# Two norm factors from running sums, and the work around them, in a hybrid decoder step on one core

## The chip, the cores and the metric

The kernel runs on one core of a Trainium2 chip. Its time is the device time of one execution in microseconds (us). A core has five engines with queues of their own: TensorE (PE in the rows, its weight loads PEld), VectorE (DVE), ScalarE (ACT), GpSimd (POOL) and SyncE (SP, which here only issues DMAs). Each engine takes its instructions in the order of its queue.

## The reference

One layer for 256 prompt tokens and 64 sample tokens (8 sequences of 8), 320 tokens of width 2048 in all, in fp32. Cut to what matters here:

```python
merged = sigmoid(gate_a) * y_a + sigmoid(gate_b) * y_b
x  = x + gt1 * rms_norm(merged @ w_o, g_post_mix)
h2 = rms_norm(x, g_pre_mlp) * (1.0 + sc2) + sh2
u  = relu(h2 @ w_up)
x  = x + gt2 * rms_norm((u * u) @ w_down, g_post_mlp)
# rms_norm(x, g): x * rsqrt(mean(x * x) + 1e-6) * g
# sh1, sc1, gt1, sh2, sc2, gt2: six parts of silu(c) @ w_ada + b_ada, for each sequence
```

Between `merged @ w_o` and `h2 @ w_up` there are two norms, one after the other: the first gives a factor r for each token (over the product with `w_o`), and the second a factor r2 (over the new x, which holds r).

## The kernel before

Activations lie transposed, with channels on the 128 partitions and the 320 tokens along a row. A matrix product is made by `gemm`: 256 output channels at a time into two PSUM banks of the pool `acc` (four banks), with 8 blocks of 128 input channels to one DMA of 1 MB (`load_w`, on SP, three buffers `raw`). Each half of such a load is split into a high part (`whi`, ScalarE) and the rest (`wlo`, VectorE), three buffers each, and each block takes three matmuls (`mm3`), so that a group of 16 blocks is 96 matmuls of 320 columns.

The order of every engine's queue is fixed when the kernel is built, by a planner that weighs its own estimates of time and the order of the program text. `tc.issue_after(ins)` keeps the instructions of a block behind `ins`, where they are on the same engine as `ins`; it bears on no other engine.

**The adaLN parts** (`ada_gen`, `ada_steps`) come in 96 steps of one 1 MB load and 8 matmuls with 32 columns of weights (`aux<-raw,cT`). After each fourth step the sums are copied (`adarow`, ScalarE), turned by four transposes and reduced (`ada_turn`). 14 of the 96 steps are left when the product with `w_o` ends. All 14 belong to `gt2`, which is not needed before the last part of the MLP. 10 of them are called in one row behind the product with `w_o`, with loads into the pool `fraw` (three buffers); the others are called by `tick` in the MLP.

**The end of the mixer.** For each of the eight groups of `w_o`, `out_squares` squares the two blocks and adds them to `ssum`, `out_tile` multiplies by `gt1` (`zg`) and turns the blocks by transposes into two PSUM banks of the pool `aux`, and `out_store` copies them to `zt` (tokens on partitions: two tiles of 128 prompt tokens, one of 64 sample tokens). The sums of squares are those of the product before `gt1` and the gain. Behind the last group `tok_rstd` adds `ssum` over the partitions with matmuls and gives r (`rstd_of`: Ln and Exp on ScalarE, then one Newton step of four small instructions on VectorE).

**Between mixer and MLP.** Six instructions make `x1 = zt * r + x1` on VectorE, 1024 wide, and ScalarE squares each half behind it with a running sum. From the six sums comes r2. `h2_scale` then multiplies blocks of 256 channels by r2 into `zt` on VectorE. A loop over eight pairs of channel blocks turns each by transposes (`aux<-ident,zt`), applies scale and shift (`h2t`, ScalarE, VectorE and GpSimd), and splits it into `gh` and `gl`, the inputs of the product with `w_up`.

**The end.** In the last of eight rounds of the MLP, each group of `w_down` is added to `za` and goes through the same `out_squares`, `out_tile` and `out_store`. `tok_rstd` gives the last r, and twelve instructions on VectorE (512 wide, L1417) make the result, each followed by its output DMA on SP's or ScalarE's queue.

## Time and profile before

| | |
|---|---|
| time, median of 3 runs | 2158.01 us (2155.7 to 2158.17) |
| time of the profiled execution | 2156.86 us |
| its span, first to last instruction | 2155.0 us |
| what lies around the span | 1.86 us |
| mean granted TensorE clock | 0.990 of full speed |
| TensorE busy | 97% of the span |
| VectorE, ScalarE, GpSimd busy | 50%, 40%, 8% |
| DMA | 401.69 MB, mean 186 GB/s |

Times inside the trace are us from the start of the span. A busy share is the share of the time in which an engine has an instruction under way; matmuls are pipelined, and the length of one (0.31 us) is longer than the distance between two (0.147 us). The granted clock of 1.00 is 2.4 GHz and 0.50 is 1.2 GHz.

### The profile page before, as it was taken

The page shows a single profiled execution, that of the slowest core. Times are in us where ns is not written, and L with a number is a line of the kernel's source. Part 1 is how long each engine was busy: PE and PEld are TensorE (multiplying, and loading weights), DVE is VectorE, ACT ScalarE, POOL GpSimd, SP SyncE. Part 2 cuts the span into 40 slices and gives each one's busy share as a digit, 9 for nine tenths or more (in the row PEclk, how much of TensorE's full clock was granted, in tenths as well). Part 3 has the DMA queues.
Part 4 walks back from the last instruction along what each step waited for, and adds up shares of the span by engine and source line. Part 5 has one row for each costly group of instructions (what it writes and reads, how often), then busy time and mean ns, then how long its engine had stood idle before and what let it go on. Part 6 is the DMA issues. An engine that isn't in the chain of part 4 may idle for free.

```text
span 2155.0 us, 34660 instructions
## 1 busy us (share of the span) xinstructions
PE 2098.8 (97%) x14605; PEld 1899.2 (88%) x14605; DVE 1077.7 (50%) x1673; ACT 863.4 (40%) x1312; POOL 165.5 (8%) x167
## 2 busy tenths in 40 slices
PE   6999998999999999999999899999999999999997
PEld 4788988557878889999999599999999999999996
DVE  3655754446765645533544643444444444444455
ACT  5322443334545434333343543434343333333343
POOL 0000100203221211000010000000000000000001
PEclk9999999999999999999999799999999999999998
DMA  9876544544766768766854565445445445445442
GB/s 310 313 268 235 195 169 130 217 129 139 241 214 225 243 208 280 227 208 203 274 178 137 180 189 176 152 145 157 145 149 156 144 150 157 143 151 157 142 152 70
DMA packets 327572, 401.69 MB, mean 186 GB/s; under 512 B 10984, under 2 KB 265528, under 8 KB 324600
## 3 DMA queue, kind: packets, MB, share of 16 engines
q1 hardware_dynamic: 301576, 362.82, 52.4%
q0 software_dynamic: 3584, 21.50, 2.8%
q10 hardware_dynamic: 22256, 15.16, 2.3%
q8 instruction: 115, 1.88, 0.4%
q14 instruction: 41, 0.34, 0.1%
HBM read 387.44 MB, written 12.01 MB: 185 GB/s over the span
## 4 chain that ended last, share of the span: by engine, by line
PE 87%; issue 4%; DVE 4%; DMA 3%; ACT 1%; SPq 1%; POOL 0%; DVEq 0%; ACTq 0%; POOLq 0%
PE acc L136 76%; PE aux L136 7%; PE aux L139 4%; DVE wlo L148 1%; DMA raw<-in_w_ada_dram 1%; DMA raw<-in_w_in_dram 1%; ACT whi L151 1%; DMA raw<-in_w_q_up_dram 1%; SPq L161 0%; DVE zu L1417 0%; DVE X L148 0%; DMA raw<-in_w_kv_up_dram 0%; POOL qt L142 0%; DVE zg L142 0%; DVE bb L967 0%
## 5 line engine op out<-in xcount | busy, mean ns | idle before, releaser
L148 DVE TENSOR_TENSOR wlo<-raw,whi 128x1024 fp32r<-128x1024 f32 (+1 forms) x493 | 604.1, 1231 | 709.1 <-ACT whi L151 708.4
L151 ACT CAST whi<-raw 128x1024 fp32r<-128x1024 f32 (+1 forms) x493 | 503.0, 1026 | 817.9 <-PE acc L136 680.5
L136 PE MATMUL acc<-hh,whi 128*128 128x320 f32 x1168 | 369.6, 317 | 2.8 <-ACT hh L151 1.5
L136 PE MATMUL acc<-hl,whi 128*128 128x320 f32 x1168 | 361.9, 310 | 0.0
L136 PE MATMUL acc<-hh,wlo 128*128 128x320 f32 x1168 | 361.7, 311 | 0.0
L136 PE MATMUL acc<-uh,whi 128*128 128x320 f32 x1024 | 316.7, 309 | 0.0
L136 PE MATMUL acc<-gh,whi 128*128 128x320 f32 x1024 | 316.7, 309 | 0.0
L136 PE MATMUL acc<-gh,wlo 128*128 128x320 f32 x1024 | 316.6, 309 | 0.0
L136 PE MATMUL acc<-gl,whi 128*128 128x320 f32 x1024 | 316.3, 309 | 0.0
L136 PE MATMUL acc<-uh,wlo 128*128 128x320 f32 x1024 | 316.1, 309 | 0.0
L136 PE MATMUL acc<-ul,whi 128*128 128x320 f32 x1024 | 316.1, 309 | 0.0
L136 PEld LDWEIGHTS acc<-hh,whi 128*128 128x128 f32 x1168 | 219.4, 188 | 34.8 <-issue 18.6
L136 PEld LDWEIGHTS acc<-hh,wlo 128*128 128x128 f32 x1168 | 219.1, 188 | 3.0 <-DVE wlo L148 1.7
L136 PEld LDWEIGHTS acc<-hl,whi 128*128 128x128 f32 x1168 | 219.7, 188 | 2.0 <-DVE hl L148 1.2
L136 PEld LDWEIGHTS acc<-gh,whi 128*128 128x128 f32 x1024 | 192.5, 188 | 1.9 <-ACT u L1387 0.8
L136 PEld LDWEIGHTS acc<-uh,whi 128*128 128x128 f32 x1024 | 192.6, 188 | 1.7 <-ACT u L1386 0.8
L136 PEld LDWEIGHTS acc<-gh,wlo 128*128 128x128 f32 x1024 | 192.6, 188 | 0.2
L136 PEld LDWEIGHTS acc<-gl,whi 128*128 128x128 f32 x1024 | 192.6, 188 | 0.0
L136 PEld LDWEIGHTS acc<-ul,whi 128*128 128x128 f32 x1024 | 192.4, 188 | 0.0
L136 PEld LDWEIGHTS acc<-uh,wlo 128*128 128x128 f32 x1024 | 192.4, 188 | 0.0
L136 PE MATMUL aux<-raw,cT 128*32 128x512 f32 (+1 forms) x832 | 116.2, 603 | 16.6 <-DVE tt L142 11.3
L145 POOL TENSOR_TENSOR ssum<-ssum,sqt 128x320 f32<-128x320 f32 x26 | 25.9, 997 | 981.2 <-ACT sqt L1267 980.3
(425 smaller groups left out, 2551.1 us busy)
## 6 DMA issues: line engine op xcount, KB each, us to landing
raw<-in_w_ada_dram SPq DMA_DIRECT2D x96, 1024.0 KB, 6.1
raw<-in_w_up_dram SPq DMA_DIRECT2D x64, 1024.0 KB, 5.7
raw<-in_w_down_dram SPq DMA_DIRECT2D x64, 1024.0 KB, 5.3
raw<-in_w_in_dram SPq DMA_DIRECT2D x60, 1024.0 KB, 5.5
raw<-in_w_o_dram SPq DMA_DIRECT2D x16, 1024.0 KB, 5.3
raw<-in_w_in_dram SPq DMA_DIRECT2D x20, 512.0 KB, 6.2
raw<-in_w_b_out_dram SPq DMA_DIRECT2D x8, 1024.0 KB, 6.4
raw<-in_w_a_out_dram SPq DMA_DIRECT2D x8, 1024.0 KB, 5.5
```

What stands on the lines that cost most here:

```text
L136: pe_last[0] = nc.tensor.matmul(out, lhsT=lhsT, rhs=rhs, start=start, stop=stop)
L139: pe_last[0] = nc.tensor.transpose(out=out, in_=in_, identity=ident[:k, :k])
L145: (eng or nc.vector).tensor_tensor(out=out, in0=a, in1=b, op=ALU.add)
L148: return (eng or nc.vector).tensor_tensor(out=out, in0=a, in1=b, op=ALU.subtract)
L151: nc.scalar.copy(out=hi, in_=src)
```

## The change

The second norm needs the sum of (x + r z)² over the channels, where z is the gated product. The changed kernel gets it as sum x² + 2 r sum xz + r² sum z². Sum x² is kept from the first norm of the layer (`xms`). `out_sums` forms the other two in each group of `w_o`, straight from the PSUM banks: three products on VectorE with a reduction, and three squares on ScalarE with a running sum. So r2 follows from r by a few instructions that are three columns wide, and the residual `x1` is made in blocks of 256 channels inside `h2_scale`, behind r2; the scaling of two of its three tiles goes to ScalarE. `h2_scale` runs one pair ahead and not two.

In the last group of `w_o` and of `w_down`, `gemm` finishes the one output block before it takes up the other (`apart`), and the last block's squares are not added to `ssum` but go into the sum over partitions by three more matmuls. Of the ten adaLN steps, three stand behind the product with `w_o` (their matmuls behind those of r), four in the loop over the pairs, and three more than before in the MLP. `behind_of` keeps their copies and reductions behind the norm's instructions, and the first weight splits of `w_up` (VectorE's half) behind r2. At the end, the samples' addition is made by TensorE: the identity times x1 plus a diagonal matrix of r times z in PSUM, which ScalarE copies out; VectorE keeps the eight prompt instructions. All prompt outputs go out on SP's queue and the samples' on ScalarE's.

```diff
+    def behind_of(i):
+
+        return tc.issue_after(i.ins) if i is not None else nullcontext()
...
-    def gemm(w2d, kt0, nkt, c0, xh, xl, fine=False):
+    def gemm(w2d, kt0, nkt, c0, xh, xl, fine=False, apart=False, floor=None):
 
         ps = [bank(acc), bank(acc)]
         for r0 in range(0, nkt, 8):
             raw, rv = load_w(w2d, kt0 + r0, 8, c0, 256)
+            if apart and r0 == nkt - 8:
+                sp = [split_w(rv, 4 * s, 4, 256) for s in range(2)]
+                for m in range(2):
+                    ms = slice(m * P, (m + 1) * P)
+                    for k in range(8):
+                        hv, lv = sp[k // 4]
+                        mm3(ps[m][:, 0:N], hv[:, k % 4, ms], lv[:, k % 4, ms], xh[:, r0 + k], xl[:, r0 + k],
+                            r0 + k == 0, k == 7)
+                tick()
+                continue
             for s in range(2):
-                hv, lv = split_w(rv, 4 * s, 4, 256)
+                with behind_of(floor if r0 + s else None):
+                    hv, lv = split_w(rv, 4 * s, 4, 256)
...
+            with behind_of(pinned[0]):
+                nc.vector.tensor_reduce(out=m9[:, 0:nb], axis=AX.X, op=ALU.add,
+                                        in_=p2[:, 0:nb * P].rearrange("p (j g u) -> p j u g", g=4, u=32)[:, :, 0:9])
...
+                    with behind_of(after_mm[0]):
+                        mm(ps[32 * (k % 4):32 * (k % 4 + 1), 0:nb * P], cT[:, r0 + k], rv[:, k], r0 + k < 4, r0 + k >= KF - 4)
...
+                    with behind_of(pinned[0]):
+                        nc.scalar.copy(out=row[:, 0:nb * P], in_=ps[:, 0:nb * P])
...
+            if f == KF - 1:
+                return t
...
-    def tok_rstd(pl, ssum):
+    def tok_rstd(pl, blocks):
+
         ps = bank()
-        for i, t0, n in TOK:
-            mm(ps[0:n, i:i + 1], ssum[:, t0:t0 + n], ones[:, 0:1], True, True)
         xx = pl.tile([P, 3], F32, name="trx")
         tm = pl.tile([P, 3], F32, name="trt")
         r = pl.tile([P, 3], F32, name="trr")
         nc.vector.memset(xx, 1.0)
-        mean_eps(xx[:, 0:2], ps[:, 0:2], D)
-        mean_eps(xx[0:NS, 2:3], ps[0:NS, 2:3], D)
+        for j, sq in enumerate(blocks):
+            for i, t0, n in TOK:
+                mm(ps[0:n, 3 * j + i:3 * j + i + 1], sq[:, t0:t0 + n], ones[:, 0:1], True, True)
+            for n, c0, c1 in ((P, 0, 2), (NS, 2, 3)):
+                if j == 0:
+                    mean_eps(xx[0:n, c0:c1], ps[0:n, c0:c1], D)
+                else:
+                    nc.vector.scalar_tensor_tensor(out=xx[0:n, c0:c1], in0=ps[0:n, 3 + c0:3 + c1], scalar=1.0 / D,
+                                                   in1=xx[0:n, c0:c1], op0=ALU.mult, op1=ALU.add)
...
+        prod = zp.tile([P, 3, 256], F32, name="prod")
+        zsq = zp.tile([P, 256], F32, name="zsq")
+        cz = zp.tile([P, 2, 3, 9], F32, name="cz")
+        nc.vector.memset(prod, 0.0)
+        nc.vector.memset(cz, 0.0)
+
+        def out_sums(bk, g, m0, m1, col):
+
+            fs = slice((2 * g + m0) * P, (2 * g + m1) * P)
+            w = slice(0, (m1 - m0) * P)
+            for i, t0, n in TOK:
+                v = bk[0][:, m0:m1, i] if i < 2 else bk[1][0:NS, m0:m1]
+                xv, pv, qv = (t.rearrange("p (m c) -> p m c", c=P) for t in
+                              (x1[i][0:n, fs], prod[0:n, i, w], zsq[0:n, w]))
+                mul(pv, v, xv)
+                nc.scalar.activation(out=qv, in_=v, func=AF.Square, accum_out=cz[0:n, 1, i, col:col + 1])
+            nc.vector.tensor_reduce(out=cz[:, 0, :, col], in_=prod[:, :, w], axis=AX.X, op=ALU.add)
...
-            ps = gemm(w_o, 0, KF, 256 * g, mh, ml)
+            last = g == 7
+            ps = gemm(w_o, 0, KF, 256 * g, mh, ml, apart=last)
             bk = out_banks()
             for m in range(2):
-                out_squares(zp2, ps[m][:, 0:N], 2 * g + m, ssum)
-            for m in range(2):
-                out_tile(zp2, ps[m][:, 0:N], 2 * g + m, m, GT1, bk)
+                lsq = out_squares(zp2, ps[m][:, 0:N], 2 * g + m, ssum)
+                if last and m:
+                    r = tok_rstd(zp, (ssum, lsq))
+                    r_exp, after_mm[0] = last_exp[0], pe_last[0]
+                if last or m:
+                    for mm_ in range(m if last else 0, m + 1):
+                        out_tile(zp2, ps[mm_][:, 0:N], 2 * g + mm_, mm_, GT1, bk)
+                if last:
+                    out_sums(bk, g, m, m + 1, 7 + m)
...
-        r = tok_rstd(zp, ssum)
+            if not last:
+                out_sums(bk, g, 0, 2, g)
+        pinned[0] = r_exp
         araw[0] = fraw
-        for _ in range(10):
+        for _ in range(3):
             next(ada_steps)
-        araw[0] = wraw
-        ssq2 = zp.tile([P, 3, 2], F32, name="ssq2")
+        after_mm[0] = None
+
+        cs = zp.tile([P, 2, 3], F32, name="cs")
         xx2 = zp.tile([P, 3], F32, name="xx2")
         r2 = zp.tile([P, 3], F32, name="r2")
         t2_ = zp.tile([P, 3], F32, name="t2_")
-        nc.vector.memset(ssq2, 0.5)
-        for i, t0, n in TOK:
-            for j in range(2):
-                fs = slice(j * D // 2, (j + 1) * D // 2)
-                nc.vector.scalar_tensor_tensor(out=x1[i][0:n, fs], in0=zt[i][0:n, fs], scalar=r[0:n, i:i + 1],
-                                               in1=x1[i][0:n, fs], op0=ALU.mult, op1=ALU.add)
-                nc.scalar.activation(out=zt[i][0:n, fs], in_=x1[i][0:n, fs], func=AF.Square,
-                                     accum_out=ssq2[0:n, i, j:j + 1])
-        add(xx2, ssq2[:, :, 0], ssq2[:, :, 1])
-        mean_eps(xx2, xx2, D)
-        rstd_of(xx2, t2_, r2)
+        nc.vector.tensor_reduce(out=cs, in_=cz, axis=AX.X, op=ALU.add)
+        mul(xx2, cs[:, 1], r)
+        nc.vector.scalar_tensor_tensor(out=xx2, in0=cs[:, 0], scalar=2.0, in1=xx2, op0=ALU.mult, op1=ALU.add)
+        mul(xx2, xx2, r)
+        nc.vector.scalar_tensor_tensor(out=xx2, in0=xx2, scalar=1.0 / D, in1=xms, op0=ALU.mult, op1=ALU.add)
+        nc.vector.tensor_scalar(out=xx2, in0=xx2, scalar1=EPS, scalar2=None, op0=ALU.max)
+        r2_last = rstd_of(xx2, t2_, r2)
+        pinned[0] = r2_last
...
-                nc.vector.tensor_scalar(out=zt[i][0:n, fs], in0=x1[i][0:n, fs], scalar1=r2[0:n, i:i + 1], scalar2=None,
-                                        op0=ALU.mult)
+                with behind_of(r2_last):
+                    nc.vector.scalar_tensor_tensor(
+                        out=x1[i][0:n, fs], in0=zt[i][0:n, fs], scalar=r[0:n, i:i + 1], in1=x1[i][0:n, fs],
+                        op0=ALU.mult, op1=ALU.add)
+                if i == 0:
+                    nc.vector.tensor_scalar(out=zt[i][0:n, fs], in0=x1[i][0:n, fs], scalar1=r2[0:n, i:i + 1],
+                                            scalar2=None, op0=ALU.mult)
+                else:
+                    nc.scalar.activation(out=zt[i][0:n, fs], in_=x1[i][0:n, fs], func=AF.Copy, scale=r2[0:n, i:i + 1])
 
         h2_scale(0)
-        h2_scale(2)
...
-            if q0 + 4 < KF:
-                h2_scale(q0 + 4)
+            if q0 + 2 < KF:
+                h2_scale(q0 + 2)
...
+            if q0 % 4 == 2:
+                next(ada_steps)
+        pinned[0] = None
+        araw[0] = wraw
...
-                ps = gemm(w_up, 0, KF, c * 1024 + 256 * g, gh, gl)
+                ps = gemm(w_up, 0, KF, c * 1024 + 256 * g, gh, gl, floor=r2_last if c + g == 0 else None)
...
-                ps = gemm(w_down, 8 * c, 8, 256 * g, uh, ul)
+                ps = gemm(w_down, 8 * c, 8, 256 * g, uh, ul, apart=last and g == 7)
...
-                        out_squares(ml2, za[:, f], f, ssum)
+                        lsq = out_squares(ml2, za[:, f], f, ssum)
+                        if f == KF - 1:
+                            r = tok_rstd(ml1, (ssum, lsq))
+                        out_tile(ml2, za[:, f], f, m, GT2, bk)
                 if last:
-                    for m in range(2):
-                        out_tile(ml2, za[:, 2 * g + m], 2 * g + m, m, GT2, bk)
                     out_store(bk, zt, g)
-        r = tok_rstd(ml1, ssum)
+
+        ysb = [bank(acc) for _ in range(4)]
+        for q in range(4):
+            mm(ysb[q][0:NS], ident[0:NS, 0:NS], x1[2][0:NS, q * 512:(q + 1) * 512], True, False)
+        dg = ml1.tile([NS, NS], F32, name="dg")
+        nc.scalar.activation(out=dg, in_=ident[0:NS, 0:NS], func=AF.Copy, scale=r[0:NS, 2:3])
         for q in range(4):
             fs = slice(q * 512, (q + 1) * 512)
-            for i, t0, n in TOK:
+            mm(ysb[q][0:NS], dg, zt[2][0:NS, fs], False, True)
+            for i, t0, n in TOK[0:2]:
                 nc.vector.scalar_tensor_tensor(
                     out=zt[i][0:n, fs], in0=zt[i][0:n, fs], scalar=r[0:n, i:i + 1],
                     in1=x1[i][0:n, fs], op0=ALU.mult, op1=ALU.add)
-                dst = y_prompt[0, t0:t0 + n, fs] if i < 2 else y_sample.rearrange("b t d -> (b t) d")[:, fs]
-                (nc.sync if i % 2 else nc.scalar).dma_start(out=dst, in_=zt[i][0:n, fs])
+                nc.sync.dma_start(out=y_prompt[0, t0:t0 + n, fs], in_=zt[i][0:n, fs])
+            nc.scalar.copy(out=zt[2][0:NS, fs], in_=ysb[q][0:NS])
+            nc.scalar.dma_start(out=y_sample.rearrange("b t d -> (b t) d")[:, fs], in_=zt[2][0:NS, fs])
```

`out_squares` and `out_store` are otherwise as before; in the groups 0 to 6 `out_sums` stands behind `out_store`. `rstd_of` now returns its last instruction, and in the first norm of the layer `ssq` is replaced by `xms`, which outlives it.

## Rows read from the trace of the kernel before

**Rows 1.** The page's busy time, share of the span and instructions of each engine.
```profile
PE 2098.8 (97%) x14605; PEld 1899.2 (88%) x14605; DVE 1077.7 (50%) x1673; ACT 863.4 (40%) x1312; POOL 165.5 (8%) x167
```

**Rows 2.** Timeline, w_o to MLP: start us, us, engine, line, instruction, count, idle before.
```profile
1185.43 0.31 PE L136 MATMUL acc<-mh,wlo 128*128 128x320 f32 x1
...
1191.22 1.06 PE L136 MATMUL aux<-raw,cT 128*32 128x512 f32 x8
...
1191.97 7.25 DVE L1334 SCALAR_TENSOR_TENSOR x<-zt,trr,x 128x1024 f32<-128x1024 f32 x6
...
1200.32 1.94 PE L136 MATMUL aux<-raw,cT 128*32 128x512 f32 x8 [0.78 <-DMA raw<-in_w_ada_dram]
...
1201.91 0.16 DVE L142 TENSOR_TENSOR r<-r,t__11359 128x3 f32<-128x3 f32 x1
...
1205.87 5.04 PE L139 MATMUL aux<-ident,zt 128*128 128x128 f32 x16
...
1214.33 0.63 PE L136 MATMUL acc<-gh,whi 128*128 128x320 f32 x1
...
1224.03 2.35 PE L139 MATMUL aux<-ident,zt 128*128 128x128 f32 x12
```

**Rows 3.** Chain that ended last, same stretch: start us, us, what.
```profile
1192.35 7.93 DMA raw<-in_w_ada_dram
```

**Rows 4.** Windows, product matmuls alone: stretch, us, TensorE busy (count), clock, DMA.
```profile
1214.00:1226.39 12.39, 4.65 (x18) 0.79 0.00 0
1226.39:1240.00 13.61, 13.61 (x93) 1.00 0.37 111
```

**Rows 5.** Windows: us, busy of PE, PEld, DVE, ACT, POOL, clock, DMA, GB/s.
```profile
1195.00:1195.50 0.50, 0.27 (x4) 0.00 (x0) 0.50 (x1) 0.50 (x2) 0.00 (x0) 0.69 1.05 397
...
1215.00:1220.00 5.00, 5.00 (x22) 2.85 (x21) 2.29 (x7) 1.91 (x3) 0.45 (x1) 0.59 0.00 0
```

**Rows 6.** Groups by line and shape, 1185 to 1240: busy us, mean ns, idle before.
```profile
L1365 ACT ACTIVATE h2t<-aux,mod 128x256 f32<-128x256 f32 x16 | 8.8, 564 | 10.9 <-PE aux L139 10.7 <-DVE gl L148 0.2
...
L148 DVE TENSOR_TENSOR gl<-h2t,gh 128x640 fp32r<-128x640 f32 x8 | 6.4, 815 | 1.6 <-ACT h2t L1365 1.3 <-ACT gh L151 0.4
L148 DVE TENSOR_TENSOR wlo<-raw,whi 128x1024 fp32r<-128x1024 f32 x5 | 6.1, 1222 | 6.2 <-ACT whi L151 6.2
L151 ACT CAST gh<-h2t 128x640 fp32r<-128x640 f32 x8 | 5.8, 721 | 0.4 <-POOL h2t L145 0.4
L1345 DVE TENSOR_SCALAR zt<-x,r 128x256 f32<-128x256 f32 x16 | 5.3, 352 | 0.0
L151 ACT CAST whi<-raw 128x1024 fp32r<-128x1024 f32 x5 | 5.2, 1049 | 3.9 <-PE acc L136 3.9
...
L142 DVE TENSOR_TENSOR h2t<-aux,mod 128x64 f32<-128x64 f32 x16 | 3.4, 223 | 8.3 <-ACT h2t L1365 8.2
```

**Rows 7.** Windows as in rows 5, the eight groups of w_o.
```profile
1066.00:1185.70 119.70, 119.70 (x819) 116.13 (x811) 49.59 (x71) 48.41 (x77) 12.87 (x14) 1.00 0.56 176
```

**Rows 8.** ScalarE's waits, 1066 to 1186: us in total, times, longest.
```profile
ACT whi L151 <- PE acc L136: 43.7, 23, 2.5
```

**Rows 9.** Chain that ended last, the kernel's end.
```profile
2133.33 5.15 PE acc L136 x35
...
2141.21 0.58 PE aux L136 x6
...
2143.33 0.75 DVE zu L1417
...
2144.74 6.62 DVE zu L1417 x10
```

**Rows 10.** Windows as in rows 5, the kernel's end.
```profile
2148.00:2151.00 3.00, 0.00 (x0) 0.00 (x0) 3.00 (x6) 0.00 (x0) 0.00 (x0) 0.50 0.98 332
```

**Rows 11.** Timeline, two single instructions elsewhere.
```profile
492.23 1.98 PE L136 MATMUL aux<-Ss,ckvs 64*128 64x512 f32 x4
...
2133.70 0.27 ACT L1288 COPY zu<-aux 128x128 f32<-128x128 f32 x1 [0.86 <-DVE zu L1287]
```

16 lines of the change are left out of this document (7 added, 9 removed).

## The prediction

> **What bounds the kernel now.** I read the page first, then the chain that ended last, then windows and timeline of the two places that the change touches. TensorE is busy 97% of the span, VectorE and ScalarE half of it or less [rows 1]; so an edit can pay only where TensorE stands still or runs at its lower clock. There are two such places. The reader is to see in the timeline [rows 2] that the last matmul of `w_o` ends at 1185.74 (I call this T), that the residual on VectorE runs from 1191.97 to 1199.2, that r2 is ready at 1202.07 (T+16.3), the first transposes of the MLP's input come at 1205.87 and the first matmul of `w_up` at 1214.33 (T+28.6). TensorE has the adaLN steps as filling, but the chain goes through their loads, 7.93 us of it [rows 3], and the steps do not hold the clock: it falls from 1.00 to 0.50 in the half microsecond at 1195, 9.4 us after the last product matmul, and comes back only within 1215 to 1220, when `w_up` matmuls run again [rows 5]. What that costs is in the timeline: an adaLN step takes 1.94 us and not 1.06, a transpose 5.04/16 = 0.32 and not 2.35/12 = 0.20 [rows 2].
>
> A mark makes before and after comparable: the first 96 matmuls of `w_up`, the 48 transposes and ten adaLN steps all done. By 1226.39 (T+40.65) 18 of the 96 were issued; the other 78 at 13.61/93 = 0.146 us [rows 4] take 11.4. **Before, the mark is at T+52.0.** At full clock this work is ten steps at 1.06, 48 transposes at 0.20, 96 matmuls at 0.146 and some twenty small ones at 0.15: 37.2 us. So 14.8 us are lost, the most that this stretch can give back.
>
> The second place is the end. The last `w_down` matmul is done at 2138.48 (E); the last r is used from 2143.33 (E+4.85); the twelve additions follow 0.66 apart [rows 9], and the span ends at 2155.0, 11.7 us behind r. DMA is at 0.98 of its engines there, with 332 GB/s [rows 10].
>
> **The change, part by part. Sums in the groups of `w_o`.** No row shows these shapes, so I draw lines through those that are there [rows 2, 6]. VectorE takes 0.223 for 64 columns and 0.815 for 640, which gives 0.42 for 256; three products and a reduction over 768 columns (0.95) are 2.2 us a group. ScalarE takes 0.72 for 640 and 1.05 for 1024, hence 0.39 for 256; from PSUM with a scale it took 0.56, and I take that with 0.2 for reading the sum: 2.3 us a group. A group lasts 119.7/8 = 15.0 us with VectorE and ScalarE busy 6.2 and 6.1 [rows 7], so there is room. The cover is the splits' lead: ScalarE's splits wait 43.7 us for buffers that TensorE frees [rows 8], a split is done 1.05 + 1.22 us behind that, and TensorE has two more buffers, 48 matmuls or 7.0 us, before it needs it. Slack 4.7 us against 2.3: I cost this at nothing; without cover it would be up to 2.3 us in each of eight groups, 18 us.
>
> **The chain to r2.** One block of the last group is finished 24 matmuls (3.5 us) early, so its work lies under the other's. Behind T: square of the last block 0.6, three matmuls 0.3 (six took 0.58 [rows 9]), two small VectorE instructions, Ln, Exp and four more at about 0.2 with their handover [rows 2]: r at T+2.8. Beside it, gate and transposes until T+1.7, then products and squares of the last block. These read the same PSUM bank by turns: a ScalarE copy there waited 0.86 us for VectorE's [rows 11]. Six at about 0.35 and the reduction 0.45 make T+4.3 (side by side it would be T+3.3). Six three-column instructions, Ln, Exp and four more at 0.2 follow: T+6.7; with 0.3 for queues r2 is at **T+7.0**, against T+16.3. That is where the residual's 7.2 us and the squares behind it went. Most of the r chain is hidden under that of the sums.
>
> **The pairs.** The residual by 256 columns: 1024 took 1.21 each, 512 took 0.66 [rows 2, 9], so 256 takes 0.38. With one scaling (0.35) the first transposes start at T+7.8. To the first `w_up` matmul it takes six transposes (0.95 for the last three at half clock), two `h2t` at 0.56, 0.22, GpSimd's addition (taken at twice that), 0.72 and 0.82 for the split [rows 6]: 4.3, and with six handovers 5.5. **T+13.3**, against T+28.6. From there each pair costs VectorE 3 x 0.38 + 0.35 + 2 x 0.22 + 0.82 + half a `wlo` 0.61 = 3.4 us, ScalarE two scalings and two `h2t` at 0.56, 0.72 and half a `whi` 0.52 = 3.5 us, TensorE six transposes, twelve matmuls and half an adaLN step = 3.5 us at full clock. All three are level: the moved scaling and the residual, which were in a stretch of their own, now make VectorE and ScalarE as long as TensorE. Seven more pairs at 3.5 are 24.5; the last pair's matmuls 1.8. The low clock: it fell 9.4 us behind T and rose within 5 us of the first `w_up` matmuls [rows 5]; here this is T+9 to T+18, in which TensorE would fall some 2 us behind. The mark also holds three adaLN steps that now run in the MLP, 3.2 us. Together 7.8 + 5.5 + 24.5 + 1.8 + 2 + 3.2 = **T+44.8: 7.2 us less.** The bounds are 14.8 (nothing lost) and, with the pairs at 4.6 us for waits between three queues that are all full, 7 x 1.1 = 7.7 lost again, so nothing gained.
>
> **The adaLN steps and SP's queue.** The first three loads are already in `fraw`. Four later ones stand in SP's queue ahead of the `w_up` loads, where ten did; at 1214 to 1226 the queue moved nothing at all [rows 4]. A load of one step has two pairs, 7 us, and needs about 3. Cost nothing; if one is late, all of TensorE's queue behind it is (3 us each).
>
> **The end.** From E to the sum over partitions (2141.21) there lie 2.7 us: additions, two squares, gate, transposes. With the first block done early there remain one addition (0.5) and one square (0.5); one more small VectorE instruction comes on top: r 1.5 us earlier. VectorE's additions fall from 12 x 0.66 = 8.0 to 8 x 0.66 = 5.3 us, but 2.62 MB at 332 GB/s are 7.9 us: DMA takes over what VectorE gives up, so I take 0.5 of the 2.7. The samples' way, four matmuls of 512 columns on 64 rows at 0.5 (1.98 for four [rows 11]), at the low clock 1.0, and four copies of about 0.6, is no longer than the prompts'. The four identity matmuls need all four banks of `acc`; were they ahead of the sum in the queue they would cost up to 2 us. **End: 2.0 less**, between 0 and 3.5.
>
> A page of the Trainium skill sees this otherwise: "DMA: Bandwidth & Descriptors", "Where 436 GB/s comes from", gives the ceiling as 435 GB/s. By that figure the output would take 6.0 us, an estimate, and the end would give about 3.5 to 4. The row with 0.98 of the engines at 332 GB/s speaks against it for these stores.
>
> Sum: 7.2 + 2.0 = 9.2. The profiled execution's span of 2155.0 becomes 2145.8, its time 2156.86 becomes 2147.7. The median shown is 1.15 above that execution, so the forecast against it is 2158.0 - 9.2 = **2148.8 us**.
>
> **The rivals.** *Nearly ideal:* the waits are short or the clock does not fall, since the quiet stretch is shorter. For it: TensorE has work nearly all the time until T+5, and `w_up` comes 15 us sooner. Against it: 9.4 us of adaLN matmuls did not keep the clock [rows 2, 5]. The 2 us come back and the pairs overlap better: 11 to 13 in the junction and 3 at the end, 2143.
>
> *VectorE and ScalarE become the bound of the pairs:* three level queues with a chain across all of them. For it: 3.4 and 3.5 us each and a shorter lead of one pair; before, they had 0.4 and 1.1 us less. At 4.4 us or more per pair the junction gives 0 to 1 and the end 2: 2155 to 2156.
>
> *The low clock stays (slower):* with one `w_up` group open, product matmuls are only half of TensorE's time in the loop. If the clock is held at 0.50 to the end of the loop, the pairs cost TensorE twice 3.5, 7 us, and the mark moves out by 7 x 3.5 - 2 = 22: 2148.8 + 22 = 2171. The gain is gone once three to four of the pairs run so (11.2/3.5). Against it: the clock rose in a mix of transposes and few product matmuls at 1215 to 1220 [rows 5]. [...]
>
> *The sums delay the splits (slower):* if the by-turns reading of the PSUM bank stretches 4.5 us of queue beyond the 4.7 us of slack, each group of `w_o` loses; from 1.2 us a group the whole gain is gone, at 2 us the time is 2165. Rows 7 and 8 speak against it.
>
> **How the numbers follow.** A measurement of this kernel can tell 0.2%, 4.3 us, from no change. Forecast (5 to 12 us less): 0.56. Nearly ideal (over 12): 0.14. The bound of the vector engines (within 4.3, or little more): 0.19. Low clock 0.05, delayed splits 0.06; half of these two still end within 0.2%. Faster 0.72, same 0.20, slower 0.08. The range goes from 2142 (two thirds of the nearly ideal case) to 2156 (that of the vector engines): it leaves out about 0.05 below and 0.12 above.
>
> **What would show it.** r2 about T+7, the first `gh` matmul about T+13; the eight `h2t` pairs 3.5 us apart with ScalarE and VectorE near full; a clock of 0.50 from about T+9 to T+18; in `w_o` TensorE still at 1.00 of each window with splits as early; the last r at E+3.3 and DMA at 0.9 or more behind it until the end. I am wrong if the pairs are 4.5 us apart, if the clock stays low, if product matmuls of `w_o` wait for `whi` or `wlo`, or if the last DMA starts no sooner.

## Result: slower by a quarter of a per cent

The changed kernel takes 2159.76 us (median of 20 runs, 2157.1 to 2166.94); the kernel before, in 20 runs beside it, 2155.47. The ratio over all runs is 1.0025 [1.0017, 1.0033], 5.4 us more; the medians are 4.3 us apart. I had forecast 2148.8 us and faster. Two things are to be explained: where the gain of the junction (the stretch from `w_o` to the MLP) went, and what was lost besides.

Three lengths (us) are compared below. T is the end of the last `w_o` matmul, W the start of the first `w_down` matmul, L the start of the last `w_down` matmul; T lies 119.0 us behind the first `w_o` matmul in every profile. A ratio is to the runs of before beside the same kernel, with its 95% interval; the lengths are those of one profile each, so they show where time went in one execution, and the ratio what it comes to over all. The time up to that first `w_o` matmul, where all kernels have the same queues, varies between 1066.2 and 1074.0 us from execution to execution, so a single span tells little. Before again and after again are the second profiles, g2_before_again and g4_after_again.

| profile | ratio to before | T to W | W to L | L to end | r2 at |
|---|---|---|---|---|---|
| before | | 97.2 | 855.6 | 16.4 | T+16.3 |
| before again | | 92.1 | 855.6 | 16.4 | T+16.3 |
| after | 1.0025 [1.0017, 1.0033] | 92.3 | 861.2 | 16.8 | T+9.8 |
| after again | | 94.2 | 861.2 | 17.0 | T+11.4 |
| e1_old_end | 1.0005 [0.9991, 1.0018] | 94.2 | 859.7 | 16.4 | T+11.4 |
| e2_only_end | 1.0015 [1.0000, 1.0030] | 92.0 | 857.1 | 20.1 | T+16.3 |
| e3_no_floor | 1.0012 [0.9998, 1.0025] | 88.3 | 861.2 | 19.5 | T+11.2 |
| e4_old_order | 1.0018 [1.0006, 1.0030] | 91.8 | 859.7 | 19.4 | T+11.5 |
| f1_junction_no_floor | 1.0010 [0.9997, 1.0022] | 89.9 | 859.7 | 16.5 | T+12.7 |
| f2_f1_last_sum_on_pe | 0.9998 [0.9985, 1.0011] | 90.0 | 859.7 | 15.6 | T+12.7 |
| f3_f2_samples_on_pe | 1.0009 [0.9998, 1.0020] | 88.4 | 859.7 | 18.3 | T+11.2 |
| f4_f1_later_splits | 1.0000 [0.9988, 1.0013] | 89.0 | 859.7 | 16.5 | T+10.6 |
| g1_before_last_sum_on_pe | 0.9997 [0.9988, 1.0005] | 91.8 | 855.6 | 15.6 | T+16.3 |
| g3_f2_hold_clock | 0.9986 [0.9975, 0.9997] | 87.0 | 859.7 | 15.6 | T+12.7 |
| h1_old_junction_hold | 0.9993 [0.9981, 1.0004] | 92.4 | 855.6 | 15.6 | T+16.5 |
| h2_hold_five_steps | 0.9985 [0.9973, 0.9996] | 91.0 | 856.9 | 15.6 | T+12.7 |
| h3_hold_six_steps | 0.9988 [0.9976, 1.0000] | 93.1 | 855.6 | 15.6 | T+12.7 |
| k1_f2_chain_first | 0.9973 [0.9961, 0.9984] | 87.7 | 859.7 | 15.6 | T+10.1 |
| k2_k1_hold_clock | 0.9986 [0.9974, 0.9998] | 87.4 | 859.7 | 15.6 | T+9.9 |
| k3_reduce_behind_r2 | 0.9970 [0.9958, 0.9983] | 86.0 | 859.7 | 15.6 | T+9.0 |

**The junction after.** The page's busy line shows no change that matters against [rows 1]:

```profile
PE 2106.7 (98%) x14633; PEld 1905.8 (88%) x14633; DVE 1088.0 (50%) x1714; ACT 874.9 (41%) x1375; POOL 170.1 (8%) x167
```

The timeline of after, to be read against [rows 2], with T at 1187.0:

```profile
1186.90 1.05 ACT L155 CAST whi<-raw 128x1024 fp32r<-128x1024 f32 x1 [0.71 <-PE acc L140]
...
1188.12 0.43 ACT L1286 ACTIVATE sqt<-acc 128x320 f32<-128x320 f32 x1
...
1189.34 1.04 PE L140 MATMUL aux<-raw,cT 128*32 128x512 f32 x2
...
1190.32 0.55 PE L143 MATMUL aux<-ident,zg 128*128 128x128 f32 x3
...
1192.77 0.58 ACT L349 COPY adarow<-aux 128x512 f32<-128x512 f32 x1 [0.50 <-PE aux L140]
1193.25 0.27 ACT L1350 ACTIVATE zsq<-aux 64x128 f32<-64x128 f32 x1
...
1196.68 0.16 DVE L240 TENSOR_TENSOR r<-r,t__11377 128x3 f32<-128x3 f32 x1
...
1197.20 1.32 PE L140 MATMUL aux<-raw,cT 128*32 128x512 f32 x8 [2.15 <-DMA raw<-in_w_ada_dram]
...
1198.45 1.92 PE L143 MATMUL aux<-ident,zt 128*128 128x128 f32 x7
...
1205.56 0.42 PE L140 MATMUL acc<-gh,whi 128*128 128x320 f32 x1
...
1218.63 1.71 POOL L149 TENSOR_TENSOR h2t<-h2t,mod 128x128 f32<-128x128 f32 x1 [1.83 <-DVE h2t L146]
1218.86 1.21 DVE L152 TENSOR_TENSOR wlo<-raw,whi 128x1024 fp32r<-128x1024 f32 x1
...
1220.12 0.90 PE L140 MATMUL acc<-gh,wlo 128*128 128x320 f32 x2 [0.75 <-DVE wlo L152]
```

Counted from T, r2 is 6.5 us earlier than in [rows 2] and the first `w_up` matmul 10.0 us earlier. But other work stands inside the chain: a weight cast ahead of the last square (`sqt`), two matmuls of an adaLN step ahead of the last block's transposes, an `adarow` copy ahead of the last of the squares for the sums, and ahead of the first transposes of `zt` an adaLN step that waited for its load. Then VectorE's split for the second quarter of the first `w_up` group, which `floor` keeps behind r2, comes only at 1218.86, behind the pairs' work, and TensorE waits for it. The windows of that stretch show it standing still and the clock, which was back at 1.00 from 1205 on, falling a second time (columns as in [rows 5]):

```profile
1200.00:1205.00 5.00, 4.60 (x13) 1.54 (x16) 3.30 (x10) 3.25 (x8) 0.59 (x1) 0.53 0.91 334
1205.00:1210.00 5.00, 5.00 (x29) 2.20 (x23) 4.82 (x12) 4.67 (x11) 1.19 (x2) 1.00 0.01 3
1210.00:1215.00 5.00, 5.00 (x35) 4.48 (x35) 3.81 (x12) 4.07 (x10) 0.58 (x1) 1.00 0.01 3
1215.00:1220.00 5.00, 2.88 (x12) 1.51 (x12) 4.36 (x10) 3.82 (x8) 2.35 (x2) 0.84 0.00 0
1220.00:1225.00 5.00, 4.34 (x15) 3.83 (x16) 3.94 (x9) 3.67 (x7) 1.90 (x3) 0.50 0.69 204
```

TensorE was busy 2.88 of 5 us from 1215 on, and the granted clock went from 1.00 (2.4 GHz) to 0.50 (1.2 GHz). The Trainium skill, "TensorE: Matmul & The Clock Gate", "What's actually happening", has the halved clock as the state that activity releases; these rows agree.

**A second profile of before** (before again) is as telling. The same count for three kernels, the product matmuls on TensorE from T+3 to T+40 (us, busy with count, clock, DMA): before, then before again, then after.

```profile
1188.70:1225.70 37.00, 4.58 (x17) 0.68 0.58 205
```
```profile
1191.60:1228.60 37.00, 7.87 (x48) 0.86 0.57 204
```
```profile
1190.00:1227.00 37.00, 11.09 (x43) 0.82 0.44 148
```

With the rest of the 96 at 0.147 us each, the prediction's mark is at T+51.6 in the first profile of before and at T+47.1 in the second. In after it is T+47.8, and the three adaLN steps that now run in the MLP cost 4.1 us there (W to L 859.7 with the old last round, 855.6 before): T+51.9. Of four profiles with the old junction (before, before again, e2, g1) three have T to W at 91.8 to 92.1; the one that the prediction was read from is the long one. Against the usual junction the change loses 4.8 us in this profile, and 6.7 in after again, where the last of the 96 starts at T+49.6.

How common the long one is can be guessed from the mean granted clock of each run: 0.990 in the first profile of before, 0.992 in the second. Of the 153 runs of before beside the experiments (three that took 2566 us and more are left out) 57 have 0.990 or less, and they take 2159.2 us on the mean, the others 2154.2. These 5.0 us are about the 5.1 by which T to W is longer in the first profile. A run's mean does not tell where its clock was low, so that these are the executions with a long low clock in the junction fits and is not shown.

**The last round and the end.** In the last round of the MLP a group of `w_down` takes longer. The waits of TensorE between 2060 and 2140 (engine, line, releaser, us in total, times, longest), of which before has none:

```profile
PE aux L143 <- DVE zg L146: 3.0, 5, 0.6
```

VectorE's splits in the timeline are 8.61 us apart from group to group (before 8.25):

```profile
2108.11 1.23 DVE L152 TENSOR_TENSOR wlo<-raw,whi 128x1024 fp32r<-128x1024 f32 x1 [0.35 <-ACT whi L155]
...
2116.72 1.23 DVE L152 TENSOR_TENSOR wlo<-raw,whi 128x1024 fp32r<-128x1024 f32 x1 [0.35 <-ACT whi L155]
```

The cause is that `out_tile` (gate and transposes) now stands behind the first block's square and not behind both; e4 below shows it. At the end of after, against [rows 9], with L at 2140.51:

```profile
2141.44 0.47 ACT L1286 ACTIVATE sqt<-za 128x320 f32<-128x320 f32 x1 [2.65 <-DVE za L149]
2141.63 1.07 PE L140 MATMUL acc<-x,ident 64*64 64x512 f32 x2
...
2142.63 0.81 PE L140 MATMUL aux<-cst,sqt 128*128 128x1 f32 x6
...
2144.80 0.16 DVE L240 TENSOR_TENSOR trr<-trr,trt 128x3 f32<-128x3 f32 x1
...
2146.74 3.59 PE L140 MATMUL acc<-zu,dg 64*64 64x512 f32 x8
```

One of the identity products stands ahead of the squares' sum: the squares are done at 2141.91, their sum starts at 2142.63. Each of the samples' products is two instructions, 0.43 us apart; the x8 are four products. From r to the end of the span it is 12.3 us, before 11.7; windows of after:

```profile
2147.00:2149.00 2.00, 2.00 (x6) 0.65 (x5) 2.00 (x4) 0.63 (x2) 0.00 (x0) 1.00 0.94 345
2149.00:2151.00 2.00, 1.33 (x4) 0.15 (x2) 1.86 (x3) 1.25 (x3) 0.00 (x0) 1.00 0.99 268
2151.00:2153.00 2.00, 0.00 (x0) 0.00 (x0) 0.00 (x0) 0.41 (x1) 0.00 (x0) 1.00 1.07 351
```

The stores ran at 268 to 351 GB/s with the DMA engines at 0.94 and more. The 435 GB/s of the Trainium skill's "DMA: Bandwidth & Descriptors", "Where 436 GB/s comes from", are its ceiling for the SBUF ports; for transfers between HBM and SBUF, as these are, the same section has the HBM side bind at about 358. By that figure the 2.62 MB take 7.3 us, an estimate, and not the 6.0 that the prediction worked out from 435. The stores stayed under both figures; loads do not keep to the second, with 399 GB/s from 1195 to 1200 in before again (its windows stand below).

### The profile page after: what moved, and what is told of

Its sections match the earlier page's. It is cut to its first block, busy times and chain, and to the rows that moved or that the text cites. A ratio compares the mean times of both kernels' runs of the same rounds, so it can differ in the third digit from the quotient of the medians.

```text
span 2157.3 us, 34798 instructions
## 1 busy us (share of the span) xinstructions
PE 2106.7 (98%) x14633; PEld 1905.8 (88%) x14633; DVE 1088.0 (50%) x1714; ACT 874.9 (41%) x1375; POOL 170.1 (8%) x167
## 4 chain that ended last, share of the span: by engine, by line
PE 87%; issue 4%; DVE 3%; DMA 2%; ACT 1%; POOL 1%; SPq 1%; ACTq 0%; DVEq 0%; POOLq 0%
PE acc L140 77%; PE aux L140 7%; PE aux L143 3%; DMA raw<-in_w_in_dram 1%; DVE wlo L152 1%; DMA raw<-in_w_ada_dram 1%; ACT whi L155 1%; POOL X L146 0%; SPq L165 0%; DVE X L152 0%; DMA raw<-in_w_q_up_dram 0%; DVE zg L146 0%; DVE hraw L492 0%; DVE qn L523 0%; DVE bb L986 0%
```

## Experiments

**Which half of the change loses.** e1 takes after's junction with before's last round and end, e2 the reverse; e3 is after without the floor (the rule that keeps VectorE's first `w_up` splits behind r2), e4 after with gate and transposes of both blocks behind both squares.

```diff
 # e1: the old last round and end
-                ps = gemm(w_down, ..., uh, ul, apart=last and g == 7)
+                ps = gemm(w_down, ..., uh, ul)
 ...
+        r = tok_rstd(ml1, (ssum,))
 # e3
-                ps = gemm(w_up, ..., gh, gl, floor=r2_last if c + g == 0 else None)
+                ps = gemm(w_up, ..., gh, gl)
 # e4: out_tile of both blocks behind both squares, as before
-                        out_tile(ml2, za[:, f], f, m, GT2, bk)
                 if last:
+                    for m in range(2):
+                        out_tile(ml2, za[:, 2 * g + m], 2 * g + m, m, GT2, bk)
                     out_store(bk, zt, g)
```

> The changed kernel up to the last round of the MLP, with the last round and the end of the kernel before. Theory (the places add up): the stretch between mixer and MLP gives about 1 to 2 us, the last round of w_down costs 2 us in the changed kernel because the transposes of each group wait for the gate on VectorE, and the end gives nothing because the stores are bound by DMA. Then a group of the last round takes 8.25 us again and not 8.6, the stretch from the first matmul of w_o to the end of the span shrinks by about 2 us against the changed kernel (1089.3 to 1087) and lies 1 us below the kernel before (1088.3). Rival (the front): the 1.3 us by which w_o began later in the changed kernel belong to the change (the moved tile shifts what lies behind it in memory); then w_o begins at 1068 here too and the time stays above that of the kernel before.

> The kernel before with the last round and the end of the changed kernel (the last group block by block, gate and transposes in the loop over the two blocks, the last squares in the sum on TensorE, the samples' addition on TensorE). Theory (the places add up): 2 us slower than the kernel before, all of it in the seven groups of the last round (8.6 us a group against 8.25); from the last product matmul to the end 16.5 us as in both. w_o begins at about 1066.7. Rival (my forecast): the end gives 2 us and the round costs nothing, so 2 us faster than before.

> The changed kernel without the rule that keeps VectorE's half of the first w_up splits behind r2. Theory (late splits): in the changed kernel only about 45 of the first 96 matmuls of w_up are issued when the last pair is done, since the second weight split of VectorE comes only at 1218.9, behind seven pairs; with that split early, 75 or more are issued by then, the clock does not fall a second time (at 1218 in the changed kernel), and the dense part begins with 4 to 5 us less left to do, at the price of r2 coming 1.2 to 2.5 us later: 3 us faster than the changed kernel. Rival (VectorE is full anyway): the split only takes its 1.2 us from the pairs and the sums, the loop ends as much later, and nothing is gained.

> The changed kernel with the gate and the transposes of both blocks behind both blocks' squares in the last round, as before; the rest of the end as changed. Theory (order in the last round): a group falls from 8.6 to 8.25 us, the last product matmul comes 2 us earlier counted from the first matmul of w_o (1070.8 against 1072.8), and the kernel is 2 us faster than the changed one. Rival (something else in the round, such as ScalarE's or VectorE's load): the group stays at 8.6 us.

Measured: ratios and lengths in the table. e1 gives W to L back its 1.5 us and the end 16.4, but is no faster than before. Its rival, that the changed kernel reaches `w_o` later, is not borne out: the first `w_o` matmul comes at 1068.6 in e1, but at 1066.7 and 1069.6 in the two profiles of before, and at 1066.2 in f4 with the same front as e1. e2 loses 1.5 us in the last round, as expected, and 3.7 at the end, which nothing had foreseen: there the clock fell, and the samples' products took twice the time. Its timeline:

```profile
2147.39 7.03 PE L140 MATMUL acc<-zu,dg 64*64 64x512 f32 x8
...
2154.45 0.58 ACT L1451 COPY zu<-acc 64x512 f32<-64x512 f32 x1 [1.13 <-PE acc L140]
```

The last copy comes 15.7 us behind L (2138.8), and L to end is 20.1. e4 shows that the order of gate and squares is worth 1.5 us of W to L. In e3 TensorE does not stand still again and the clock stays up:

```profile
1210.00:1215.00 5.00, 5.00 (x35) 4.28 (x32) 3.62 (x10) 3.06 (x7) 0.81 (x2) 1.00 0.01 3
1215.00:1220.00 5.00, 5.00 (x34) 4.53 (x35) 4.47 (x12) 5.00 (x11) 0.80 (x2) 1.00 0.00 0
```

T to W is 88.3, against 92.3 and 94.2 with the floor.

e4 has the same junction as after, and in its profile the stretch from r2 to the first `w_up` matmul ran at another clock. The windows of that stretch, after and then e4:

```profile
1196.83:1205.56 8.73, 7.95 (x30) 2.80 (x31) 6.69 (x20) 4.92 (x11) 0.59 (x1) 0.61 0.91 336
```
```profile
1199.63:1205.95 6.32, 5.04 (x30) 1.77 (x22) 6.20 (x19) 4.53 (x10) 0.59 (x1) 1.00 1.03 374
```

The same 30 matmuls (16 of adaLN steps, 14 transposes) take 8.7 us at a clock of 0.61 and 6.3 at 1.00. The two differ in one thing more: the adaLN step that waits for its load begins 0.4 us behind r2 in after and 0.4 ahead of it in e4.

**Putting the good parts together.** f1 is e1 without the floor; f2 adds the last squares' sum on TensorE and the last group block by block; f3 adds the samples on TensorE to f2; f4 is f1 with the third and fourth split kept behind r2's exponential.

```diff
 # f2 on f1
-                ps = gemm(w_down, ..., uh, ul)
+                ps = gemm(w_down, ..., uh, ul, apart=last and g == 7)
 ...
+                        if f == KF - 1:
+                            r = tok_rstd(ml1, (ssum, lsq))
 # f4 on f1
-                with behind_of(floor if r0 + s else None):
+                with behind_of(floor if r0 else None):
```

> The kernel after, with before's last round and end and without the floor on the first w_up splits. My theory: the floor made the weight splits late and cost the junction about 4 us, the last round 2 us, the end up to 3 us. Then from the last w_o matmul to the first w_down matmul 88 to 91 us (after: 92.3), a group of the last round 8.25 us, from the last w_down matmul to the end 16.4 us; time 2153, 2 to 3 us less than before, ratio 0.998 to 0.999. Rival (the w_up matmuls were not late, the one profile without the floor was only lucky with its clock): 92 to 94 us there and the time of e1, 2157, ratio 1.000.

> f1, and at the end only the last squares' sum on TensorE and the last w_down group half by half; the samples' addition stays on VectorE, the projections in their old order. My theory: r is 0.8 to 1.5 us earlier and the stores follow it, so from the last w_down matmul to the end 15.2 to 15.9 us in place of 16.4, and the time 0.5 to 1 us less than f1. Rival (the transfers bound the end whenever r comes): 16.4 us again and the time of f1.

> f2, and the samples' last addition on TensorE as the kernel after has it, the projections still in their old order. My theory: the eight diagonal matmul instructions take 0.43 us each at the full clock and 0.86 at half of it, the clock falls behind the last w_down matmul in most executions, and the last stores wait for them: from the last w_down matmul to the end 19 to 20 us, the time 3 to 4 us more than f2. Rival (the matmuls are covered by the other stores): 15 to 16.5 us and the time of f2.

> f1 with only the splits of the first w_up group's second half (its third and fourth) kept behind the exponential of the second factor. My theory: one 1 us cast on ScalarE and one split on VectorE leave the chain of the factor, which ends about 1 us earlier (T+10.3 in place of T+11.3, T being the end of the last w_o matmul), the first w_up matmul 1 us earlier too, the matmuls behind are not held: time 0.5 to 1 us less than f1. Rival (the later split holds the matmuls as the floor of the kernel after did): the time of the kernel with the floor, 3 to 4 us more than f1, and TensorE waits for VectorE's split past T+30.

The lengths came as my theory had them (f1 89.9, f2 15.6 at the end, f4 89.0 and r2 2 us earlier), but the time of f1 did not fall under that of before: the theory that floor, order and samples were all of the loss is wrong. f3 against f2 is 0.0011 or 2.4 us, known to 0.0017; L to end is 2.7 us longer in its profile. That is the price of the samples on TensorE, shown by the profile and not by the ratio alone. How much the floor costs on average stays open. Three pairs differ by it alone (after and e3, e4 and f3, e1 and f1): their profiles differ by 3.5 to 6.0 us between T and L, their ratios by -0.0013, -0.0009 and +0.0005, each known to 0.0015 to 0.0018.

**Is it the profile of before?** g2 and g4 are before and after once more, g1 is before with the last sum on TensorE alone. g3 adds 30 matmuls whose sums nobody reads to f2.

```diff
 # g3, behind the three adaLN steps
+        hold = bank()
+        for k in range(30):
+            with behind_of(after_mm[0]):
+                mm(hold[:, 0:N], mh[:, k % KF, 0:P], mh[:, (k + 1) % KF], k == 0, k == 29)
```

> The kernel before, with the last group of w_down half by half and the last squares' sum on TensorE, and nothing else. My theory: the end pays 0.8 us of its own whatever the junction is, so from the last w_down matmul to the end 15.6 us in place of 16.4 and a time 0.8 us less, ratio 0.9995 to 0.9999. The junction is before's, so the profile is also one more sample of it: from the last w_o matmul to the last w_down matmul 947 to 950 us if the 952.9 of before's profile was an execution with a long low clock, 952 to 953 if that is its usual length (rival).

> The kernel before, unchanged, profiled once more. My theory (the stretch at the lower clock behind w_o differs from execution to execution, and the profile of before had a long one): from the last w_o matmul to the last w_down matmul 947 to 951 us, and from the start to the first w_o matmul another length than 1066.7 too. Rival (before's profile was typical): 952 to 953 us.

> f2 with 30 more matmuls of 320 columns on mh, whose sums nobody reads, on TensorE behind the first adaLN steps and ahead of the first transposes (4.4 us in a stretch in which it waits). My theory: the lower clock behind w_o costs the new junction 2 to 4 us; with the matmuls the clock stays at 1.00 past T+12, transposes take 0.20 us and not 0.32, T to the first w_down matmul is 86 to 88 us (f2: 90.1), the time 2 to 3 us less than f2, ratio 0.998 to 0.999. Rival (the chain over VectorE and ScalarE sets the pairs, TensorE's clock does not): 90 us again and the time of f2.

> The kernel after, unchanged, profiled once more. My theory: the late weight split and its second stretch at the lower clock are in every execution, so from the last w_o matmul to the last w_down matmul 952 to 955 us again (first profile 953.5), more than before by 2 to 6; from the last w_down matmul to the end 19 to 20 us if the clock falls before the diagonal matmuls, 16 to 17 if not. Rival (its first profile was an unlucky one): 948 to 950.

g1 and g2 have T to L at 947.5 and 947.7: the 952.9 was an execution with a long low clock. In before the clock came back behind 1218 (T+32); in before again it was back by 1210 (T+21), as its windows show:

```profile
1195.00:1200.00 5.00, 1.22 (x12) 0.16 (x8) 5.00 (x5) 3.70 (x7) 0.00 (x0) 0.89 1.05 399
1200.00:1205.00 5.00, 3.67 (x16) 0.40 (x16) 3.10 (x9) 3.61 (x8) 0.00 (x0) 0.50 1.04 382
1205.00:1210.00 5.00, 4.29 (x22) 1.64 (x18) 3.88 (x15) 0.94 (x2) 0.00 (x0) 0.58 1.02 380
```

g4 has T to L at 955.4 (after 953.5), with the two falls of after some 2 us later and a third ahead of them. g3 holds the clock at 1.00 from 1200 on (T+10) and gains the 3 us forecast in T to W; its ratio is 0.0012 below that of f2, which is known to 0.0017.

**Why is even that no more?** h1 holds the clock in the old junction (with the end of g1 and 42 such matmuls among the ten adaLN steps); h2 and h3 have five and six adaLN steps in the wait for r2, beside such matmuls, and so two and three less in the MLP.

```diff
 # h2 on f2; h3: six steps with 0, 0, 10, 6, 6, 6
-        for _ in range(3):
+        for s in range(5):
             next(ada_steps)
+            for k in range([0, 0, 10, 10, 10][s]):
+                with behind():
+                    mm(hold[:, 0:N], mh[:, k, 0:P], mh[:, k + 1], True, True)
```

> The kernel before with the last squares' sum on TensorE at the end (as the run with that alone) and 42 matmuls of 320 columns on mh, whose sums nobody reads, behind seven of the ten adaLN steps, where TensorE waits for loads. My theory: the lower clock costs the old junction too; held at 1.00, T to the first w_down matmul falls from 91.9 to 88 to 90 us, since the chain over residual and squares (first w_up matmul at T+25) stays, and the time is 2 to 4 us less than that run, 2150 to 2152, ratio 0.998 to 0.999. Rival (the low clock there lies wholly under the wait for r2, so it costs nothing): 92 us and the time of that run.

> The run with the clock held in the new junction, with five adaLN steps instead of three behind w_o, so two less in the MLP, and the 30 matmuls in three rows of ten between them. My theory: a step behind the first w_down matmul costs 1.37 us (4.1 us for three), one in the wait for r2 nothing: from the first w_down matmul to the last 857.0 us (three steps there: 859.7), T to the first w_down matmul 87 to 88, time 2 to 3 us less than with three steps, ratio 0.997 to 0.998. Rival (the loads of the two steps come late and hold the first transposes): T to the first w_down matmul 89 to 91 and the time no less.

> The same with six steps behind w_o and 28 such matmuls. My theory: from the first w_down matmul to the last 855.6 us, as before; T to the first w_down matmul 87 to 89; time 3 to 4 us less than with three steps, 2149 to 2150. Rival: the sixth step waits for its load on TensorE ahead of the transposes and gives back what it saves, the time of the run with five.

In time all three came out as the rival. In h1 the clock is 1.00 throughout and T to W stays at 92.4: in the old junction the low clock of the usual length lies under the wait for r2. In h2 and h3 W to L falls to 856.9 and 855.6, 1.3 to 1.4 us a step, but T to W is 4.0 and 6.1 longer than in g3. So the steps are not free in the new wait, at least not beside 28 to 30 filling matmuls. The rival's reason, late loads, is not in the profiles: TensorE waits for no load from 1190 to 1215 there. The steps and the filling matmuls themselves stand among the first transposes; r2 is at T+12.7 as in g3, the first `w_up` matmul at T+20.9 and T+21.6 (g3 T+19.5).

**The chain to r2.** In f2's timeline (T at 1188.1) ten adaLN matmuls, most of them at the lower clock, hold the last block's transposes, and the `adarow` copy stands ahead of two of its three squares:

```profile
1190.47 2.80 PE L140 MATMUL aux<-raw,cT 128*32 128x512 f32 x10
...
1193.20 0.90 PE L143 MATMUL aux<-ident,zg 128*128 128x128 f32 x3
...
1195.49 0.58 ACT L349 COPY adarow<-aux 128x512 f32<-128x512 f32 x1 [3.75 <-PE aux L140]
1195.97 0.28 ACT L1350 ACTIVATE zsq<-aux 128x128 f32<-128x128 f32 x1
...
1200.72 0.16 DVE L240 TENSOR_TENSOR r<-r,t__11377 128x3 f32<-128x3 f32 x1
```

k1 puts the chain first, k2 adds 25 filling matmuls to k1, k3 also keeps the adaLN reduction behind r2.

```diff
 # k1 on f2 (sum_last: the last square that out_sums issues)
-                    r_exp, after_mm[0] = last_exp[0], pe_last[0]
+                    r_exp = last_exp[0]
 ...
                 if last:
-                    out_sums(bk, g, m, m + 1, 7 + m)
+                    after_mm[0] = pe_last[0]
+                    sum_last = out_sums(bk, g, m, m + 1, 7 + m)
 ...
-        pinned[0] = r_exp
+        pinned[0] = sum_last
 # k3 on k1: the three steps are called behind the chain to r2 (copies: the pin of their adarow copy)
-                    with behind_of(pinned[0]):
+                    with behind_of(copies[0] or pinned[0]):
 ...
+        pinned[0], copies[0] = r2_last, sum_last
```

> f2 with the queues set as the prediction priced them: the adaLN matmuls stand behind the last block's transposes on TensorE and the adarow copy behind the last square on ScalarE. My theory: in f2 r2 came at T+13 and not T+7 since ten adaLN matmuls (2.8 us at the lower clock) stand ahead of these transposes and an adarow copy (0.6 us) ahead of the squares; without them r2 is at T+9 to T+10, T to the first w_down matmul 87 to 88 us (f2: 90.1), time 2 to 3 us less than f2. Rival (TensorE's work, not r2, sets the stretch): r2 earlier, yet 89 to 90 us and the time of f2.

> The same with 25 matmuls of 320 columns on mh, whose sums nobody reads, behind the second and third adaLN step. My theory: both gains add, since one is the chain to r2 and the other the clock behind it: T to the first w_down matmul 85 to 86.5 us, time 1 to 2 us less than without them, ratio to before 0.997 to 0.9985. Rival (they fill the wait that the shorter chain has just closed, and push the transposes out): 87 to 89 us and no less time.

> The run with the chain first, and also the adarow reduction kept behind r2 on VectorE (there it stood between the small instructions of r2, and in the profiled execution, at the lower clock, they waited 1.58 us behind it for TensorE's transposes). My theory: r2 at T+8 to T+9 also when the clock is low, T to the first w_down matmul 86 to 88 us, time the same as that run or up to 1.5 us less, ratio to before 0.9965 to 0.9975. Rival (that wait was only in the profiled execution): r2 no earlier than T+10, the same time within the interval.

k1 gives 0.9973 and k3 0.9970 [0.9958, 0.9983], 2150.33 us at a median of 2158.62 for before beside it: the best version, 6.5 us under before and, by way of the two ratios, about 12 under after. The 6.5 may be rather much: six of the eleven runs of before beside k3 have the low mean clock of 0.990 or less, nine of 23 beside k1, which is 5.8 us under before. k2 is no faster than k1, as the rival had it. k3's timeline, with T at 1187.2:

```profile
1188.32 0.43 ACT L1286 ACTIVATE sqt<-acc 128x320 f32<-128x320 f32 x1
...
1190.14 0.86 PE L143 MATMUL aux<-ident,zg 128*128 128x128 f32 x3 [0.52 <-ACT zsq L1350]
...
1190.93 3.33 PE L140 MATMUL aux<-raw,cT 128*32 128x512 f32 x16
...
1192.24 0.15 DVE L240 TENSOR_TENSOR trr<-trr,trt 128x3 f32<-128x3 f32 x1
...
1196.06 0.16 DVE L240 TENSOR_TENSOR r<-r,t__11349 128x3 f32<-128x3 f32 x1
```

and its product matmuls from T+3 to T+40:

```profile
1190.20:1227.20 37.00, 15.74 (x87) 0.95 0.48 163
```

87 of 96 are done, so the mark is at 40 + 9 x 0.147 + 4.1 = T+45.4, near the T+44.8 of the prediction: its sum was within reach of this code, not of the order that it judged. That the two agree so well is luck: the first `w_up` matmul of k3 comes at T+18.4 and not T+13.3, and from there to the last of the 96 it takes 22.9 us and not the 28.3 of the sum.

## Why the prediction was wrong

Four terms failed: the time that before loses, the chain to r2, the wait that `floor` adds (it has no price in the sum), and the end with the last round. Term by term:

- **"14.8 us are lost, the most that this stretch can give back."** Wrong in size: it was the loss of one execution. In before again the mark is at T+47.1, so 9.9 are lost. The low clock of [rows 5] was taken for that of every execution; by the mean clocks it may be that of about a third of them.
- **The chain to r2, T+7.0.** Mis-sized: T+9.8 and T+11.4. The cause is in the queues: weight splits on ScalarE and VectorE, adaLN matmuls, their copy and their reduction stand inside it. I had counted 0.3 for queues. k3 takes adaLN out of it and reaches T+9.0; the other 2 us are in r (T+5.2, not T+2.8), whose square starts 1.1 us behind T, behind a weight cast. A better queue is worth 0.0025 to 0.0028 of the ratio (k1 and k3 against f2, known to 0.0018), the largest single effect found.
- **From r2 to the first `w_up` matmul, 6.3 us.** Right at the full clock (e4), 8.7 and 9.0 in after and after again. The low clock came about where it was forecast, T+9 to T+18 (in after it is back by 1205, T+18), and the difference to e4 is 2.4 us, where the sum had 2. In k3 it takes 9.4 at a clock of 1.00, with adaLN matmuls and their reduction in between.
- **The pairs.** Right in rate: in after they follow each other at about 3 us (3.5 forecast). But the matmuls between them were held by the late split. The floor stood in the diff, and I gave its wait no price. A second low clock came with it; in e3 neither is there. By the profiles the floor costs 3.5 to 6.0 us between T and L; the ratios leave its mean open.
- **The adaLN loads at nothing.** Nearly right: one step waited 2.15 us for its load, ahead of the first transposes, which came at 1198.45; the first scaled block was there at 1197.90, so this is some 0.5 us at most.
- **Three adaLN steps in the MLP, 3.2 us.** 4.1 measured, 1.37 each: the sum has the 8 matmuls of a step alone, and a step also brings its share of transposes, which no run prices by itself.
- **Sums in the groups of `w_o` at nothing.** Right: 119.0 us in all profiles.
- **The end, 2.0 less.** Of the 1.5 us by which r was to come earlier, 0.2 came in after and 0.8 where nothing stood ahead of the sum (f2); the end of f2 has all of these (16.4 to 15.6). The 0.5 for VectorE's shorter additions were not gained: in after they end 5.9 us behind r, before 8.1, yet the span ends 12.3 behind r, before 11.7. What failed most is the samples' way. Four instructions in [rows 11] were read as four products and are two; a product takes 0.86 us at the full clock and 1.7 at the lower, so four take 3.59 or 7.03 us, and L to end rises to 18.3 to 20.1 where the clock has fallen. The new order of gate and squares in the last round had no price in the sum and costs 1.5 us.
- **The sum.** Against the usual before: junction 4.8, order 1.5, end 0.4 to 3.7, together 6.7 to 10 us lost by the profiles; 5.4 are measured. Before's long executions bring the two together: if 57 of 153 runs are 5.0 us longer, before's mean lies 1.9 above its usual time, which leaves 4.8 to 8.1. That is an estimate from the mean clocks, not a measurement of the junction.

None of the rivals was the case. The low clock did come back in the loop, but for some 7 us behind a wait for a split, not to the loop's end; the rival in which VectorE and ScalarE are the bound came nearest in time.

## What to carry to other kernels

A gain read as "time lost around a wait" needs a second execution before it is priced, above all where TensorE's clock falls. When a chain is shortened, list what else the queues put between its links, and pin that behind the chain: f2 and k3, the same work in another order, are 6.0 us apart by their ratios. A wait that the change adds for its own sake (a floor, a pin) is an edit with a price, also where it sits on an engine that is half idle.

## What was not expected of the hardware

The granted clock comes back at different times in the same code: behind T+32 in one profile of before, by T+21 in another, with 5.1 us between them in T to W. It fell among adaLN matmuls with 32 columns of weights in the profiles of before (where they wait for loads, 1.9 us ahead of the last) and f2, and during the last block's transposes in k3. With filling matmuls of 128 columns of weights by 320 among them it stood at 1.00 (h1 throughout, g3 once they ran); in k3 it was at 1.00 from 1195 (T+8) on without any.

GpSimd's addition of 128x128 took 0.41 to 1.71 us in after's loop, where before it took 0.41 to 0.45. In its groups by line and shape, the additions and the residual that now runs beside them:

```profile
L1398 DVE SCALAR_TENSOR_TENSOR x<-zt,trr,x 128x256 f32<-128x256 f32 x16 | 7.6, 506 | 0.0
...
L149 POOL TENSOR_TENSOR h2t<-h2t,mod 128x128 f32<-128x128 f32 x8 | 6.8, 856 | 44.3 <-DVE h2t L146 44.3
```

The Trainium skill, "SBUF — State Buffer", "Who interferes with whom", says that a VectorE instruction with two inputs in SBUF contends with a GpSimd instruction that reads SBUF. The residual has two such inputs, and the rows agree: beside one or two residuals an addition of after takes 0.58 to 0.98 us. The two longest, 1.71 and 1.39, ran beside a weight split of VectorE, which also has two (the first is in the timeline of the junction, 1218.63 beside 1218.86); in e3, where the floor is gone and no split falls there, none takes more than 0.59. No run took the residual away. I had taken it at 0.38 us; it is 0.51 on the mean.
